# Block one's attention: from part-array float32 to full-array split float32r

## The chip, the core and the metric

The kernel runs on one core of one Trainium2 chip. What counts is the device time of one execution in microseconds; the median of three runs is compared. TensorE multiplies matrices out of SBUF into PSUM, VectorE, ScalarE and GpSimd (POOL) do the elementwise work, and SyncE (SP) issues nearly all DMAs from one in-order queue.

## What is computed

A network of two blocks on 512 tokens of 1024 features. The first block has two layers, and each runs five attention branches of 4 heads with 64 features beside one another: dsa (a top-256 mask over index scores), fox (forget gates in the logits), stick-breaking (sb), nsa (compressed, selected and window keys; with these sizes the selected and the window part see all causal keys) and mem (256 memory tokens). The branches are gated, merged and projected. The second block is not touched by the change.

```python
def _masked_softmax(logits, mask):
    l = jnp.where(mask, logits, -jnp.inf)
    m = jnp.max(l, axis=-1, keepdims=True)
    m = jnp.where(jnp.isfinite(m), m, 0.0)
    e = jnp.where(mask, jnp.exp(l - m), 0.0)
    return e / jnp.maximum(jnp.sum(e, axis=-1, keepdims=True), 1e-30)

def _fox_attention(q, k, v, log_f):
    ...
        logits = (jnp.einsum('bqhd,bshd->bhqs', q_blk, k).astype(jnp.float32) * scale
                  + jnp.moveaxis(c_blk, 1, 2)[..., None] - cum_s[:, :, None, :])
        mask = (s_pos[None, :] <= t[:, None])[None, None]
        p = _masked_softmax(logits, mask).astype(v.dtype)
        return jnp.einsum('bhqs,bshd->bqhd', p, v)

def _stick_breaking_attention(q, k, v):
    ...
        z = jnp.einsum('bqhd,bshd->bhqs', q_blk, k).astype(jnp.float32) * scale
        strict = (s_pos[None, :] < t[:, None])[None, None]
        log_keep = jnp.where(strict, jax.nn.log_sigmoid(-z), 0.0)
        later = lax.cumsum(log_keep, axis=3, reverse=True) - log_keep
        a = jnp.where(strict, jnp.exp(jax.nn.log_sigmoid(z) + later), 0.0).astype(v.dtype)
        return jnp.einsum('bhqs,bshd->bqhd', a, v)

def _layer(...):
    h = _rmsnorm(x, norm_g)
    p = _split_columns(h @ w_in)
    ...
    merge = jax.nn.sigmoid(p['merge'].reshape(B, S, N_BRANCH, D_MODEL))
    merged = jnp.sum(merge * jnp.einsum('bsnc,ncd->bsnd', ys, w_branch), axis=2)
    return x + merged @ w_out
```

## The kernel before

All work is written down as calls that a planner (`Plan`, L110) records. At `flush` (L363) it orders them by priority and by estimated costs (`cost`, L186), hands `ev` copies to VectorE or ScalarE and `tt` operations to VectorE or GpSimd, and emits each engine's fixed order; slots of tagged tiles are part of the plan. In the profile nearly every operation so recorded has line L119; copies and splits have L671 to L687.

Block one (`BlockOne.layer`, L1482) goes through the branches as mem, fox, sb, nsa, dsa. In a stage it writes down the attention of one branch (`*_a`), the projections of the next (`*_p`) and the gate and merge of the one before (`zm`, L1452), and `mix` (L283) spreads the priorities of attention and the rest over the same interval, so that projections stand between the attention's steps. Block two's conditioning products (`ada`) are spread in as well.

Projections are split already: weights and activations are cut into a float32r high part and a low part, and `mm3` (L745) adds three products of 128 rows by 128 columns. For each 512 KB weight tile `wraw` (four buffers) a high part `whi` is cast and a low part `wlo` subtracted, and the buffer is loaded again only after that.

The attention is float32. `softmax_branch` (L1125) takes a query tile of 128, and for each head `head` (L1087) forms the logits from 64 rows of q and k, adds mask rows, takes max, exponential, reciprocal and scale, turns the probabilities by transposes through PSUM and copies them to `pT`. `weigh` (L1118) multiplies 64 columns of v with `pT` for two heads, whose outputs lie in the two halves of the PSUM partitions. A float32 matmul leaves two records (passes) in the trace. `sb_a` (L1198) and `nsa_a` (L1402) have their own forms, `dsa_idx` (L1239) forms index scores from 32 rows a head. q, k and v of a branch lie in tiles of tag `qkv` (six slots); work tiles of 512 columns come from `t2` (12), and logits, turned tiles and outputs share five PSUM banks (`at`, L987).

Of the kernel before, what the change touches and what calls it, by code (L numbers as in the profile page):

```python
# [132 lines left out]
class Plan:  # L133
# [4 lines left out]
    def __init__(self, tc):  # L138
# [11 lines left out]
        self.kept = set()  # L150
        self.free = {e: 0.0 for e in "tsvgy"}
# [34 lines left out]
    def cost(self, eng, name, outs, ins, a, k):  # L186
        n = max(self.size(x) for x in outs[:1] + [y for y in ins if name in ("tensor_reduce", "max")])
        if eng == "t":
# [10 lines left out]
            if ins[0].dtype == F32R:  # L199
                return max(cols / 2.4, 107.0) + 2.5  # L200
# [23 lines left out]
    def add(self, alts, name, a, k):  # L224
# [24 lines left out]
        for ap, wr in [(x, False) for x in ins] + [(x, True) for x in outs]:  # L249
# [33 lines left out]
    def mix(self, *spans):  # L283

        a, b = min(x for x, _ in spans), max(y for _, y in spans)
        for x, y in spans:
            w = [o.alts[0][2] if o.alts[0][0] == "t" else 1.0 for o in self.ops[x:y]]
            tot, c = sum(w) or 1.0, 0.0
            for o, wi in zip(self.ops[x:y], w):
                o.prio = a + (b - a) * (c + 0.5 * wi) / tot  # L290
# [13 lines left out]
    def merge(self, ops):  # L304
# [48 lines left out]
        return out  # L353

# [285 lines left out]
class Net:  # L640
# [19 lines left out]
    nt2 = 12  # L660
# [49 lines left out]
    def wraw(self, src, m, n, tag="wraw", bufs=4):  # L710
        raw = self.wp.tile([P, 1024], F32, tag=tag, name="wraw", bufs=bufs)
# [197 lines left out]

class BlockOne:  # L910
# [7 lines left out]
    def run(self, xp, layers=DEPTH):  # L918
# [3 lines left out]
        self.xs = n.dr.tile([P, KD, S], F32, name="x_keep")  # L922
        with ExitStack() as ctx:
# [5 lines left out]
            n.pos_i = self.wk.tile([P, P], I32, tag="posi", name="pos_i", bufs=1)  # L929
            nc.sync.dma_start(n.pos_i[:NT, :P], I["positions"].rearrange("o (t p) -> (o t) p", p=P))  # L930
            for t in range(NT):
                r = self.qkv("x_in").rearrange("p a b -> p (a b)")
# [23 lines left out]
            self.c_cmp = self.const("cmp")  # L956
            self.negones = bp.tile([P, P], F32, tag="negones", name="negones")
# [55 lines left out]
    def mem_prep(self, wk):  # L1013

        n, nc, bp = self.n, self.nc, self.bp
        memT = [self.qkv("memT").rearrange("p a b -> p (a b)") for _ in range(2)]
        mt = lambda k: memT[k // 4][:, (k % 4) * NMEM:(k % 4 + 1) * NMEM]
# [15 lines left out]
        self.mem_k, self.mem_v = [], []  # L1033
        for l in range(DEPTH):
            hh = [self.qkv("memh", F32R).rearrange("p a b -> p (a b)") for _ in range(4)]
            class V:
                def __init__(s, a, b): s.t = (a, b)
                def __getitem__(s, i):
                    k, ts = i[1], i[2]
                    o = (k % 4) * NMEM  # L1040
                    return s.t[k // 4][:, o + ts.start:o + ts.stop]
            h = (V(hh[0], hh[1]), V(hh[2], hh[3]))
            for k in range(KD):
                m = n.t2("memg")[:, :NMEM]
                n.ev(m, mt(k), NMEM, scale=self.vcol(l, "mem_norm", k))
                sl = slice(0, NMEM)
                n.split(h[0][:, k, sl], h[1][:, k, sl], m, NMEM)
            w = self.I["w_mem_kv"][l]
            mk = bp.tile([P, 2, NMEM], F32, tag=f"memk{l}", name="mem_k")
            mv = bp.tile([P, 2, NMEM], F32, tag=f"memv{l}", name="mem_v")  # L1050
            for c, ps in n.proj_T(w[:, :256], h, slice(0, NMEM), 256):
                n.ev(mk[:, c], ps, NMEM)
            for t, ps in n.proj(w[:, 256:512], h, 256, range(2)):
                n.ev(mv[:, t], ps, 256)
            self.mem_k.append(mk)
            self.mem_v.append(mv)


    def pT(self, nm, h, dst, scale=None):
        n = self.n  # L1060
        o = OFF[nm]
        for c, ps in n.proj_T(self.w[:, o:o + 256], h, slice(0, S), 256):
            n.ev(dst[:, c], ps, 512, scale=scale)

    def qkv(self, nm, dt=F32):
        return self.bp.tile([P, 2, S], dt, tag="qkv", name=nm, bufs=6)

    def back(self, src_tiles, dst, scale=None):

        n, nc = self.n, self.nc  # L1070
        ps = self.tp()
        for t, s in enumerate(src_tiles):
            nc.tensor.transpose(ps[:, t * P:(t + 1) * P], s, n.ident)
        n.ev(dst, ps[:, :P * len(src_tiles)], P * len(src_tiles), scale=scale)

    def rope_T(self, w, h, dst, scale=None):
# [6 lines left out]
        for c in range(2):  # L1083
            self.back([r[:, t, c * P:(c + 1) * P] for t in range(NT)], dst[:, c], scale)


    def head(self, q, k, nk, mask, extra=None, gate=None):  # L1087
# [5 lines left out]
        nc.tensor.matmul(out, q, k, start=True, stop=mask is None and extra is None)  # L1093
# [14 lines left out]
        ps = self.tp()  # L1108
        for j in range(nk):
            nc.tensor.transpose(ps[:, j * P:(j + 1) * P], p[:, j * P:(j + 1) * P], n.ident)  # L1110
        pT = n.t2("pT")
        n.ev(pT[:, :N], ps[:, :N], N)
        return pT
# [4 lines left out]
    def weigh(self, pv, c, parts):  # L1118

        for x, (v, p, K) in enumerate(parts):  # L1120
            for i in range(2):
                self.nc.tensor.matmul(pv[64 * i:64 * i + 64, c * P:(c + 1) * P], v[i], p[i], start=x == 0,
                                      stop=x == len(parts) - 1, skip_group_check=True)

    def softmax_branch(self, q, k, v, yT, nk_of, mask_of, extra=None):  # L1125
        n = self.n
        for t in range(NT):
            nk = nk_of(t)
            pv = self.pv()
            ts = slice(t * P, (t + 1) * P)  # L1130
            for c in range(2):
                pT = [self.head(q[64 * i:64 * i + 64, c, ts], k(2 * c + i, nk), nk, mask_of(t),
# [1245 lines left out]
```

## Time and profile before

| | us |
|---|---|
| median of 3 runs (3393.59 to 3395.28) | 3395.07 |
| the profiled execution's own time | 3393.83 |
| its span, first to last instruction | 3392.0 |
| mean granted TensorE clock, share of full speed | 0.981 |

The profile is of one execution. Its page gives busy time by engine; a table by stretches gives the same for a piece of the span with the granted clock and the DMA share; the order of one engine's instructions gives start and duration of each, with equal neighbours merged. Matmuls overlap, so their durations are longer than the time that they occupy the array; start plus duration is the end, and the difference of two ends is the step. A shape such as 64*128 64x512 is rows and columns of the array in use, then the moving operand. float32r shows as f32 on matmuls.

### The profile page before, as it was taken

The page shows a single profiled execution, that of the slowest core. Times are in us where ns is not written, and L with a number is a line of the kernel's source. Part 1 is how long each engine was busy: PE and PEld are TensorE (multiplying, and loading weights), DVE is VectorE, ACT ScalarE, POOL GpSimd, SP SyncE. Part 2 cuts the span into 40 slices and gives each one's busy share as a digit, 9 for nine tenths or more (in the row PEclk, how much of TensorE's full clock was granted, in tenths as well). Part 3 has the DMA queues.
Part 4 walks back from the last instruction along what each step waited for, and adds up shares of the span by engine and source line. Part 5 has one row for each costly group of instructions (what it writes and reads, how often), then busy time and mean ns, then how long its engine had stood idle before and what let it go on. Part 6 is the DMA issues. An engine that isn't in the chain of part 4 may idle for free. (4 is left out here: it accounts for less than half of the span.)

```text
span 3392.0 us, 43819 instructions
## 1 busy us (share of the span) xinstructions
PE 3266.5 (96%) x16852; PEld 2496.3 (74%) x16856; DVE 2242.3 (66%) x4343; ACT 1123.3 (33%) x2548; POOL 242.3 (7%) x234
## 2 busy tenths in 40 slices
PE   7999999999999999999987899999999999989999
PEld 7677665677777666567775787888887777668887
DVE  8475855456665766445899977555557778775654
ACT  4333433212332433222321733111114666641112
POOL 1000100000000100000121100000000101110000
PEclk9999999999999999999998899999999999999999
DMA  6231421224232322123521231233222202133422
GB/s 184 77 92 40 126 70 52 58 79 126 57 88 68 101 67 73 46 73 94 167 75 56 82 94 57 90 91 100 86 61 76 64 20 78 48 95 92 117 75 88
DMA packets 378346, 278.21 MB, mean 82 GB/s; under 512 B 12172, under 2 KB 351384, under 8 KB 377880
## 3 DMA queue, kind: packets, MB, share of 16 engines
q1 hardware_dynamic: 378136, 275.40, 27.5%
q8 instruction: 133, 2.18, 0.3%
q14 instruction: 77, 0.63, 0.1%
HBM read 265.92 MB, written 9.44 MB: 81 GB/s over the span
## 5 line engine op out<-in xcount | busy, mean ns | idle before, releaser
L119 PE MATMUL ps_mm<-h_ffn,whi 128*128 128x512 f32 (+1 forms) x2112 | 566.3, 356 | 16.0 <-ACT h_ffn L119 8.0
L671 DVE CAST whi<-wraw 128x1024 fp32r<-128x1024 f32 (+7 forms) x339 | 199.3, 588 | 547.0 <-PE ps_mm L119 529.4
L687 DVE TENSOR_TENSOR wlo<-wraw,whi 128x1024 fp32r<-128x1024 f32 (+6 forms) x395 | 425.5, 1078 | 23.1 <-ACT whi L671 9.5
L119 PEld LDWEIGHTS ps_mm<-h_ffn,whi 128*128 128x128 f32 x2112 | 375.5, 190 | 78.0 <-ACT h_ffn L119 10.4
L119 PE MATMUL ps_mm<-hh,wlo 128*128 128x512 f32 x960 | 397.7, 414 | 0.9 <-DVE wlo L687 0.9
L119 PE MATMUL ps_mm<-hl,whi 128*128 128x512 f32 x960 | 396.1, 413 | 0.0
L119 PE MATMUL ps_mm<-hh,whi 128*128 128x512 f32 x960 | 393.9, 410 | 0.0
L119 PE MATMUL ps_mm<-h_ffn,wlo 128*128 128x512 f32 (+1 forms) x1056 | 374.4, 355 | 0.0
L119 DVE TENSOR_REDUCE mx<-ps_lg 128x1 f32<-128x384 f32 (+3 forms) x288 | 146.2, 509 | 156.2 <-PE ps_lg L119 135.8
L119 DVE CUSTOM_DVE_ANT_0 ada_junk<-wraw,cond,cols 128x1024 bf16<-128x1024 f32 x160 | 214.4, 1340 | 25.5 <-DMA wraw<-in_ada_wT_dram 24.9
L119 PEld LDWEIGHTS ps_mm<-hh,wlo 128*128 128x128 f32 x960 | 181.2, 189 | 59.1 <-issue 25.7
L119 PEld LDWEIGHTS ps_mm<-hh,whi 128*128 128x128 f32 x960 | 181.2, 189 | 58.6 <-issue 27.3
L119 PEld LDWEIGHTS ps_mm<-h_ffn,wlo 128*128 128x128 f32 x1056 | 200.4, 190 | 27.5
L119 PEld LDWEIGHTS ps_mm<-hl,whi 128*128 128x128 f32 x960 | 181.3, 189 | 52.0 <-issue 21.2
L119 ACT ACTIVATE p<-ps_lg,mx 128x384 f32<-128x384 f32 (+3 forms) x288 | 156.6, 547 | 163.0 <-DVE mx L119 161.6
L671 ACT COPY pT<-ps_tp 128x384 f32<-128x384 f32 (+3 forms) x244 | 105.0, 441 | 298.7 <-PE ps_tp L119 297.6
L119 PE MATMUL ps_mm<-fhi,wlo 128*128 128x512 f32 (+1 forms) x528 | 187.5, 357 | 0.0
L119 PE MATMUL ps_mm<-flo,whi 128*128 128x512 f32 (+1 forms) x528 | 186.7, 356 | 0.0
L119 PE MATMUL ps_mm<-fhi,whi 128*128 128x512 f32 (+1 forms) x528 | 186.4, 355 | 0.0
L671 ACT COPY gpad<-ps_mm 128x512 f32<-128x512 f32 x64 | 33.4, 523 | 429.9 <-PE ps_mm L119 429.3
L671 ACT CAST whi<-wraw 128x1024 fp32r<-128x1024 f32 (+8 forms) x122 | 114.5, 940 | 175.2 <-PE ps_mm L119 111.9
L687 POOL TENSOR_TENSOR wlo<-wraw,whi 128x256 fp32r<-128x256 f32 (+4 forms) x66 | 107.7, 1634 | 878.4 <-DVE whi L671 472.3
(519 smaller groups left out, 6425.9 us busy)
## 6 DMA issues: line engine op xcount, KB each, us to landing
wraw<-in_w_in_dram SPq DMA_DIRECT2D x132, 512.0 KB
wraw<-in_ada_wT_dram SPq DMA_DIRECT2D x96, 512.0 KB
wraw<-in_ffn_w_in_dram SPq DMA_DIRECT2D x88, 512.0 KB
wraw<-in_ffn_w_out_dram SPq DMA_DIRECT2D x64, 256.0 KB
wraw<-in_w_branch_dram SPq DMA_DIRECT2D x20, 512.0 KB
wraw<-in_w_out_dram SPq DMA_DIRECT2D x16, 512.0 KB
wraw<-in_ab_w_in_dram SPq DMA_DIRECT2D x16, 512.0 KB
x_keep<-xT SPq DMA_DIRECT2D x3, 2048.0 KB
```

The source lines that it names most:

```text
L119: return plan.add([(eng, lambda: fn(*a, **k))], name, a, k)
L671: self.plan.either("tensor_copy", {"v": lambda x: x.tensor_copy(out, in_), "s": lambda x: x.copy(out, in_)}, out, in_)
L687: f = lambda x: x.tensor_tensor(out, a, b, op=op)
```

## The change

q and k of every branch are stored as a stack: for each head, 64 rows of high part and under them 64 rows of low part, in float32r. A second copy of k with the halves swapped (`swapped`, two DMAs of 128 KB a head from SBUF to SBUF) lets two products over 128 rows give all four partial products, and `head` and `sb_a` do so. v is stored as 64 high and 64 low columns, so one product over 128 columns gives both halves, and `out_pair` adds them. The turned probabilities are cut into high and low parts straight from PSUM, for two query tiles side by side (`pair`, `sets`, `weigh`); keys that only the second tile sees take 128 columns, the others 256. Index scores and compressed logits take the same form. The branches run heads outside and tile pairs inside.

Storage follows: tag `st` has 8 slots of 4 KB a partition, and a branch takes two each for q, k and v; `t2` goes from 12 to 8; mem keys and values of the second layer go to DRAM and come back, as do the index scores. `zm` is written down in two halves, one ahead of the next projections and one behind, `mix` gives attention priorities over 0.7 of the interval, and `towards` lets the planner hold a projection until its target slots are free. The planner's cost of a float32r matmul is changed as well.

```diff
-                return max(cols / 2.4, 107.0) + 2.5
+                return max(cols / 2.255, 107.0) + 2.5
...
+        if alts[0][0] == "t":
+            tiles += [x.tensor.name for x in self.into if x.tensor.name not in tiles]
...
+                o.prio = a + (b - a) * (1.0 if (x, y) != spans[0] else lead) * (c + 0.5 * wi) / tot
...
-    nt2 = 12
+    nt2 = 8
...
+    def slot(self, nm, dt=F32R):
+        return self.bp.tile([P, 2, S], dt, tag="st", name=nm, bufs=8)
...
+    def stack(self, dst, c, ps, scale=1.0):
+
+        n = self.n
+        N = ps.shape[1]
+        for i in range(2):
+            src = ps[64 * i:64 * i + 64]
+            hi = dst[c][0:64, i, :N]
+            n.ev(hi, src, N, scale=None if scale == 1.0 else scale)
+            self.nc.vector.scalar_tensor_tensor(dst[c][64:P, i, :N], src, scale, hi.bitcast(F32),
+                                                op0=ALU.mult, op1=ALU.subtract)
...
+    def split_v(self, dsts, ps):
+
+        src = ps.rearrange("p (h d) -> p h d", d=64)
+        o = 0
+        for dst in dsts:
+            H = dst.shape[1]
+            x = src[:, o:o + H]
+            self.n.ev(dst[:, :, :64], x, 64 * H)
+            self.nc.vector.tensor_tensor(dst[:, :, 64:], x, dst[:, :, :64].bitcast(F32), op=ALU.subtract)
+            o += H
...
+    def swapped(self, k1, h):
+
+        k2 = self.bp.tile([P, S], F32R, tag="k2", name="k2", bufs=3)
+        for a, b in ((0, 64), (64, 0)):
+            self.nc.sync.dma_start(k2[a:a + 64].bitcast(F32), k1[h // 2][b:b + 64, h % 2].bitcast(F32))
+        return k2
...
-        nc.tensor.matmul(out, q, k, start=True, stop=mask is None and extra is None)
+        nc.tensor.matmul(out, q, ks[0][:, :N], start=True, stop=False)
+        nc.tensor.matmul(out, q, ks[1][:, :N], start=False, stop=mask is None and extra is None)
...
+    def pair(self, t0, nk_of, head):
+
+        n = self.n
+        hl = self.parts("pT")
+        for u in range(2):
+            nk = nk_of(t0 + u)
+            src = head(t0 + u, nk)[:, :nk * P].rearrange("p (j q) -> p j q", q=P)
+            hi, lo = (x[:, :nk, u * P:(u + 1) * P] for x in hl)
+            n.ev(hi, src, nk * P)
+            self.nc.vector.tensor_tensor(lo, src, hi.bitcast(F32), op=ALU.subtract)
+        return hl, nk_of(t0 + 1), nk_of(t0)
+
+    def weigh(self, pv, i, sets):
+
+        flat = [(v, p, a) for v, hl, a in sets for p in hl]
+        for x, (v, p, a) in enumerate(flat):
+            self.nc.tensor.matmul(pv[:, i * 256 + a:(i + 1) * 256], v, p, start=x == 0, stop=x == len(flat) - 1,
+                                  skip_group_check=True)
+
+    def sets(self, v, hl, keys, full):
+        return [(v(j), [x[:, j, (0 if j < full else P):] for x in hl], 0 if j < full else P) for j in range(keys)]
 
     def pv(self):
         return self.at("ps_pv")
 
-    def weigh(self, pv, c, parts):
-
-        for x, (v, p, K) in enumerate(parts):
...
+    def out_pair(self, yT, c, t0, pv):
+
+        n, nc = self.n, self.nc
+        lo = n.t2("pv_lo")
+        nc.scalar.copy(lo[64:P], pv[64:P])
+        for i in range(2):
+            cols = slice(i * 256, (i + 1) * 256)
+            nc.vector.tensor_tensor(yT[64 * i:64 * i + 64, c, t0 * P:(t0 + 2) * P], pv[0:64, cols], lo[64:P, cols], op=ALU.add)
+
...
+    def softmax_branch(self, q, keys, v, yT, nk_of, mask_of, extra=None):
+        for c in range(2):
+            ks = [keys(2 * c + i) for i in range(2)]
+            for t0 in (0, 2):
+                pv = self.pv()
+                for i in range(2):
+                    h = 2 * c + i
+                    hl, nk, full = self.pair(t0, nk_of, lambda t, nk: self.head(
+                        self.hd(q, h)[:, t * P:(t + 1) * P], ks[i], nk, mask_of(t), extra(h, nk) if extra else None))
+                    self.weigh(pv, i, self.sets(lambda j: v[c][:, j, i], hl, nk, full))
+                self.out_pair(yT, c, t0, pv)
...
+                    hl = [x.rearrange("p j q -> p (j q)")[:, :N] for x in self.parts("sb_aT")]
+                    n.split(hl[0], hl[1], a, N)
+                    for y, x in enumerate(hl):
+                        nc.tensor.matmul(pv[i][:, s0:], v[c][:, s, i], x, start=s == NT - 1 and y == 0, stop=s == 0 and y == 1,
+                                         skip_group_check=True)
...
-                nc.tensor.matmul(lg, qi[hh * 32:hh * 32 + 32, t * P:(t + 1) * P], ki[hh * 32:hh * 32 + 32, :N],
-                                 start=True, stop=True)
+                nc.tensor.matmul(lg, self.hd(qi, hh)[:, t * P:(t + 1) * P], ki[:, :N], start=True, stop=True)
...
+            nc.sync.dma_start(self.scores[:, t, :N], sc[0])
...
+                for h in range(4):
+                    for x in range(2):
+                        nc.tensor.matmul(lg[:, h * 32:(h + 1) * 32], self.hd(q, h)[:, t * P:(t + 1) * P], kc[x], start=x == 0, stop=x == 1)
...
+            if d == 3:
+                yield
...
+            zm = self.zm(BRANCHES.index(seq[i - 1]), h, ys[seq[i - 1]], acc, i == 1) if i else iter(())
+            next(zm, None)
...
+            next(zm, None)
             if i + 1 < len(seq):
                 nx = seq[i + 1]
                 st[nx] = self.dsa_p(h, ckv) if nx == "dsa" else getattr(self, nx + "_p")(h)
...
```

## Rows read from the trace of the kernel before

**Rows 1.** The page's first part: busy us, share of the span, instructions.

```profile
PE 3266.5 (96%) x16852; PEld 2496.3 (74%) x16856; DVE 2242.3 (66%) x4343; ACT 1123.3 (33%) x2548; POOL 242.3 (7%) x234
```

**Rows 2.** Table by stretches: length, busy us (instructions), clock, DMA share, GB/s.

```profile
20.00:1612.00 1592.00, 1565.11 (x7510) 1094.94 (x7515) 966.84 (x1927) 510.43 (x1112) 100.97 (x84) 0.99 0.28 81
320.00:420.00 100.00, 96.30 (x466) 66.94 (x465) 80.77 (x152) 46.08 (x74) 14.95 (x16) 1.00 0.37 104
420.00:820.00 400.00, 397.32 (x1803) 267.79 (x1805) 217.23 (x421) 109.24 (x258) 18.05 (x12) 1.00 0.25 71
1800.00:2000.00 200.00, 168.85 (x935) 139.68 (x935) 185.97 (x409) 95.07 (x297) 16.20 (x8) 0.85 0.22 70
2640.00:3000.00 360.00, 354.18 (x2226) 258.89 (x2224) 274.71 (x767) 228.98 (x655) 43.62 (x67) 1.00 0.17 54
```

**Rows 3.** TensorE's order around 237 us: start, us, operation, tiles, shape, records merged.

```profile
236.24 0.40 PE L119 MATMUL ps_mm<-hh,wlo 128*128 128x512 f32 x1
236.56 1.12 PE L119 MATMUL ps_lg<-fox_k,fox_q 64*128 64x512 f32 x2
...
237.62 0.50 PE L119 MATMUL ps_mm<-hh,whi 128*128 128x512 f32 x1
237.95 0.40 PE L119 MATMUL ps_mm<-hl,whi 128*128 128x512 f32 x1
```

**Rows 4.** The same view around 85 us.

```profile
85.12 0.40 PE L119 MATMUL ps_mm<-hl,whi 128*128 128x512 f32 x1
85.45 0.70 PE L119 MATMUL ps_lg<-mem_k,mem_q 64*128 64x256 f32 x2
```

**Rows 5.** The same view around 524 us.

```profile
523.73 0.40 PE L119 MATMUL ps_mm<-hl,whi 128*128 128x512 f32 x1
524.06 0.87 PE L119 MATMUL ps_pv<-pT,nsa_v 128*64 128x128 f32 x10
524.86 0.50 PE L119 MATMUL ps_mm<-hh,wlo 128*128 128x512 f32 x1
```

**Rows 6.** The same view: first and last of 475 records behind a part-array matmul.

```profile
44.48 0.55 PE L119 MATMUL ps_tp<-ident,mem_in 128*128 128x128 f32 x3
...
1502.23 0.50 PE L119 MATMUL ps_br<-yh,wlo 128*128 128x512 f32 x1
```

**Rows 7.** Views of ps_lg and ps_pv: records, ns min/median/max, first and last start.

```profile
L119 PE MATMUL ps_lg<-nsa_k,nsa_q x128: 272/481/693, 446.3 to 1382.9; 64*128 64x128 f32 x32, 64*128 64x256 f32 x32, 64*128 64x384 f32 x32, 64*128 64x512 f32 x32
...
L119 PE MATMUL ps_pv<-pT,nsa_v x320: 272/273/324, 461.7 to 1400.0; 128*64 128x128 f32 x160
```

**Rows 8.** TensorE's order around 158 and 183 us, short float32r matmuls.

```profile
158.29 0.40 PE L119 MATMUL ps_mm<-hh,wlo 128*128 128x512 f32 x1
158.53 0.22 PE L119 MATMUL ps_lg<-cum_parts,pick 128*128 128x128 f32 x1
158.59 0.23 PE L119 MATMUL ps_lg<-causalb,identb 128*128 128x128 bf16 x1
158.63 0.31 PE L119 MATMUL ps_lg<-cum_parts,pick 128*128 128x128 f32 x1
...
183.03 0.28 PE L119 MATMUL ps_mm<-whi,hh 128*128 128x256 f32 x1
183.15 0.28 PE L119 MATMUL ps_mm<-wlo,hh 128*128 128x256 f32 x1
```

**Rows 9.** VectorE's order around 533 us; its weight casts up to 1650 us.

```profile
533.25 0.56 DVE L119 TENSOR_REDUCE mx<-ps_lg 128x1 f32<-128x384 f32 x1 [0.27 <-PE ps_lg L119]
533.72 0.68 DVE L687 TENSOR_TENSOR acc<-acc,gt 128x512 f32<-128x512 f32 x1
534.32 0.15 DVE L119 TENSOR_TENSOR sm<-sm,nsa_v 128x1 f32<-128x1 f32 x1
...
L671 DVE CAST whi<-wraw 128x1024 fp32r<-128x1024 f32 x128 | 89.4, 698 | 243.7 <-PE ps_mm L119 231.7 <-PE ps_br L119 9.4 <-issue 2.4
```

**Rows 10.** Waits of the SP queue: waited for, us in total, times, longest.

```profile
SPq L119 <- DVE wlo L687: 1702.2, 331, 26.6
```

More of the change, by code (lines that the diff above doesn't have):

```diff
@@ L353, in merge, with towards @@
         return out
+    def towards(self, *aps):
+        self.into = aps
     def keep(self, *aps):
@@ L1045, in mem_prep @@
                 n.ev(m, mt(k), NMEM, scale=self.vcol(l, "mem_norm", k))
-                sl = slice(0, NMEM)
-                n.split(h[0][:, k, sl], h[1][:, k, sl], m, NMEM)
+                n.split(h[0][:, k, every], h[1][:, k, every], m, NMEM)
             w = self.I["w_mem_kv"][l]
[L1049 to L1052, printed above, removed]
+            mk, mv = self.mem_tiles()
@@ L1060, in pT @@
+    def pT(self, nm, h, dst, scale=1.0):
         n = self.n
         o = OFF[nm]
+        n.plan.towards(dst[0])
         for c, ps in n.proj_T(self.w[:, o:o + 256], h, slice(0, S), 256):
[L1063 to L1070, printed above, removed]
+            self.stack(dst, c, ps, scale)
+            n.plan.towards(*dst[1 + c:])
@@ L1083, in rope_T, with head @@
         for c in range(2):
-            self.back([r[:, t, c * P:(c + 1) * P] for t in range(NT)], dst[:, c], scale)
-    def head(self, q, k, nk, mask, extra=None, gate=None):
+            n.plan.towards(dst[c])
+            self.stack(dst, c, self.turn([r[:, t, c * P:(c + 1) * P] for t in range(NT)]), scale)
+        n.plan.towards()
+    def head(self, q, ks, nk, mask, extra=None, gate=None):
         n, nc, wk = self.n, self.nc, self.wk
@@ L1107, in head, with parts @@
         n.scale_rows(p, sm)
[L1108 to L1113, printed above, removed]
+        return self.turn([p[:, j * P:(j + 1) * P] for j in range(nk)])
+    def parts(self, nm):
+        return [self.wk.tile([P, 4, 2 * P], F32R, tag=x, name=nm, bufs=self.nparts) for x in ("ph", "pl")]
+    nparts = 2
+    def pair(self, t0, nk_of, head):
[8 more added lines that the diff above has]
+        return hl, nk_of(t0 + 1), nk_of(t0)
@@ L1202, in sb_a @@
         for c in range(2):
-            pv = self.pv()
-            off = [0, 512, 896, 1152]
-            at = [wk.tile([P, 1280], F32, tag="sba", name="sb_a", bufs=2) for _ in range(2)]
+            k2 = [self.swapped(k, 2 * c + i) for i in range(2)]
+            pv = [self.pv() for _ in range(2)]
             later = [n.t2("sb_later") for _ in range(2)]
@@ L1244, in dsa_idx @@
         wi = bp.tile([P, NT, 4], F32, tag="wi", name="idx_w")
-        qr = wk.tile([P, NT, 256], F32, tag="rq", name="idx_r", bufs=1)
+        qr = [n.t2("idx_r").rearrange("p (h c d) -> p h c d", h=4, c=4) for _ in range(NT)]
+        kr = wk.tile([P, NT, 256], F32, tag="rq", name="idx_kr", bufs=1)
         for t, ps in n.proj(self.w[:, o:o + 292], h, 292, range(NT)):
@@ L1304, in dsa_kv @@
             n.tt(r[:, t].rearrange("p (h d) -> p h d", d=64), a, b, ALU.add, 256)
-            n.ev(v[:, t], ps[:, 256:], 256)
+            self.split_v([x[:, t] for x in v], ps[:, 256:])
         for c in range(2):
-            self.back([r[:, t, c * P:(c + 1) * P] for t in range(NT)], k[:, c])
+            n.plan.towards(k[c])
+            self.stack(k, c, self.turn([r[:, t, c * P:(c + 1) * P] for t in range(NT)]))
+        n.plan.towards()
         return k, v
@@ L1523, in layer @@
                 plan.spread(self.topk, self.topk[0], a0)
-        self.zm(BRANCHES.index(seq[-1]), h, ys[seq[-1]], acc, False)
+        for _ in self.zm(BRANCHES.index(seq[-1]), h, ys[seq[-1]], acc, False):
+            pass
         mh = bp.tile([P, KD, S], F32R, tag="hh", name="mh")
```

320 lines of the change are left out of this document (181 added, 139 removed).

## The prediction

> **What bounds the kernel now.** I read the page's first part, then the table by stretches, then TensorE's order of work. TensorE is busy 96% of the span, VectorE 66%, ScalarE 33% [rows 1]. The change touches block one alone, which runs from about 10 us to 1612 us: there TensorE is busy 1565 of 1592 us at a granted clock of 0.99, which is its 2.4 GHz level, while VectorE is busy 967 and ScalarE 510 [rows 2]. So block one is bound by TensorE's own work, and its time changes with that work as long as the other engines keep feeding it.
>
> What that work costs is read from ends of matmuls, not from their durations, which overlap: the step from the end of one record to the end of the next. Full-array projections of 512 columns step by 0.23 us (from 238.12 to 238.35) [rows 3]. The old attention is dearer than its arithmetic in three ways.
>
> - Logits run on 64 rows in float32, two passes each. The pair with 512 columns ends 1.04 us after the projection before it (236.64 to 237.68) [rows 3], the pair with 256 columns 0.63 us after (85.52 to 86.15) [rows 4]. So 256 columns more cost a pair 0.41 us, 512 columns 0.82, and about 0.22 is the price of entering.
> - After such a pair the next projection of 512 takes 0.44 us and not 0.23 (237.68 to 238.12) [rows 3]. After a run of 64-column products of probabilities and values (ps_pv) it is the same: 0.43 us (524.93 to 525.36) [rows 5].
> - A run of 10 ps_pv passes takes 0.80 us (524.13 to 524.93) [rows 5], entering included, with the two heads' column halves side by side.
>
> Such an exit to the full array occurs 475 times, from 44.5 us to 1502.2 us [rows 6].
>
> **What the change removes.** There are 384 logit passes (nsa 128, and mem, fox, dsa and stick-breaking 64 each, by rows of the same view as [rows 7]), 192 pairs: 40 each of 128, 384 and 512 columns, 72 of 256. On the line through the two measured pairs they cost 0.42, 0.63, 0.84 and 1.05 us: 16.8 + 45.4 + 33.6 + 42.0 = 138 us. The 896 ps_pv passes (nsa 320 [rows 7], fox and dsa 160 each, mem 128, stick-breaking and compressed nsa 64 each), their steps summed over all records, take 130 us. The index scores (48 passes) and compressed logits (64) take 26 us in the same count. The 475 exits at 0.19 us, the mean over all of them, are 89 us. Sum: 383 us.
>
> **What it puts in their place on TensorE.** Every product becomes a full-array float32r one, so entries and exits go. Steps: 0.23 us for 512 columns [rows 3], 0.12 for 256 [rows 8], 0.176 for 384 on the line between. For 128 columns there are two prices: 0.06 us where a long matmul stands before (158.69 to 158.75) and 0.11 to 0.12 where a short one does (158.82 to 158.94) [rows 8]; I take 0.115, since the new ones come in runs. The Trainium skill ("TensorE: Matmul & The Clock Gate", "LDWEIGHTS") says a weight load takes its columns over 1.2, an estimated 0.107 us for 128, which would bind such runs; the rows behind short matmuls agree, and by the rule the sum stays as it is made below and the 16 us of its lower bound don't come.
>
> Per layer: logits are two products a tile, 2 x (0.115 + 0.12 + 0.176 + 0.23) = 1.28 us a head, for 20 causal heads (fox, dsa, stick-breaking 4 each, nsa 8) 25.6; mem 32 x 0.12 = 3.8; index 4 x 0.53 = 2.1; compressed 32 x 0.115 = 3.7. Values, two query tiles at once: a causal head has 8 products of 256 columns and 4 of 128, 1.42 us, for 16 heads 22.7; mem 3.8; stick-breaking 4 x 1.28 = 5.1; compressed 1.0. Twelve more transposes for the index at 0.11: 1.3. That is 69 us a layer, 138 in both. Bounds: at 0.06 for all 288 products of 128 columns it is 16 us less; the dear end is the sum itself, because no full-array row shows more. Net: 383 - 138 = **245 us less TensorE work**.
>
> **What it adds elsewhere.** A VectorE instruction on 512 columns occupies the engine 0.60 us (533.72 to 534.32), on 384 0.47 (533.25 to 533.72) [rows 9]; on that line 0.34 for 256 and 0.20 for 128. Per layer: low parts of probabilities, 16 x 1.61 + 16 x 0.34 = 31 us; low parts of q and k, 16 tensor halves x 2 x 0.60 = 19, with nsa and mem keys 22; of v 6; stick-breaking's split 10; the two-half adds on the way out 13; index and compressed parts 8. About 90 us a layer, 180 in both; some may go to ScalarE or GpSimd. ScalarE gains about 20 a layer. So VectorE has 967 + 180 = 1147 us to do beside 1592 - 27 - 245 = 1320 us of TensorE work, of which 89 us of weight casts can move to ScalarE [rows 9]. All of this lies beside TensorE's work; without that cover 1147 us is still less than 1320.
>
> Hidden altogether: the copies of swapped halves (12 heads a layer in fox, stick-breaking and dsa, two copies of 128 KB each) and of mem keys, values and scores, some 6 MB a layer where 81 GB/s at a share of 0.28 flow now [rows 2]. They queue on SP with the weight loads, and SP mostly waits for the low-part subtraction of weights (1702 us in all, longest 26.6) [rows 10]. Behind a copy that waits for VectorE's stack stand weight loads, and behind those the projections; four raw buffers, each 24 products of 0.23 = 5.5 us, are the cover. The new order of the merge (half ahead of the next projections, attention at 0.7 of the stage) costs no instruction.
>
> **The waits that come back.** This is the unknown. TensorE's idle share against VectorE's busy share: 0.7% at 54%, 1.7% at 61%, 1.6% at 76%, 15.6% at 93% (there the clock also fell to 0.85 of 2.4 GHz) [rows 2]. Block one would stand at 76 to 83%, and unevenly: a stretch at 81% today (320 to 420 us) [rows 2] gains VectorE work and loses TensorE work. I take 5.5% of 1320 + waits, about 75 us, where 27 are now: 48 us given back. The ends are 0 and the 15.6% row, 1320 x 0.185 = 244 - 27 = 217.
>
> So the span falls by 245 - 48 = 197. The profiled execution took 3393.83 us for a span of 3392.0, 0.04% under the median of 3395.07; 3393.8 - 197 = **3197 us**.
>
> **The rivals.** *VectorE becomes the bound* in the attention stages. For it: 81% at 320 to 420 us already, one in-order queue in which a new subtraction stands behind weight subtractions over 1024 columns, and a transposed tile that now stays in PSUM until two readers are done. Against: the average of 76 to 83%. Price: waits as at 1800 to 2000 us, 217 more, so a gain of 28 and 3366 us; from 131 us more on, 3280, I count it as this rival. By the Trainium skill ("TensorEngine Tiling (Array Packing)", "PSUM Bottleneck") a faster TensorE can make the PSUM copies the bottleneck; no row here shows it on this stage, and it would act as this rival does.
>
> *The copies block SP.* Each of 24 heads' swapped keys waits for a stack, and the weight loads behind starve the projections. The change ends slower once a head's copy costs more than 245/24 = 10.2 us of idle TensorE; with 20 us, below SP's longest wait of 26.6 [rows 10], it is 3393.8 - 245 + 480 = 3629 us. Against: raw buffers cover 22 us of projection, and SP's wait is mostly room, not need.
>
> *Nothing comes back*: waits stay at 27 us and 128-column products hide their loads: 3393.8 - 261 = 3133 us.
>
> **How the numbers follow.** Forecast 0.75 (3150 to 3280), VectorE bound 0.14 (3280 to 3370), nothing back 0.07 (3133 to 3150), SP blocked 0.04 (above 3400). The range 3145 to 3285 takes in the forecast and the near edges of its neighbours. Faster by over 0.2% (6.8 us, about what a measurement of this kernel tells from no change): 0.95; within 0.2%: 0.01; slower: 0.04.
>
> **What would show it.** Right: no records of 64 rows or 64 columns under ps_lg, ps_z and ps_pv before block two; a projection right behind ps_pv stepping 0.23; block one ending near 1415 us; TensorE idle there for 60 to 90 us, before projections that wait for wlo and before transposes that wait for p. VectorE busy there about 1100 us. Wrong: VectorE above 90% over 300 us with TensorE idle beside it, or TensorE waiting for swapped keys. A 128-column float32r run stepping well off 0.115, or a full-array product that keeps an exit of 0.19 behind it, would make the sum itself wrong.

## The result, and the profile after

The changed kernel takes 3293.5 us (median of four runs, 3291.6 to 3294.7) against 3394.7 for the kernel before on the same chip: a ratio of 0.970, 95% interval 0.9685 to 0.9718. It is faster by 101 us where 197 were forecast, and lies 8.5 us above the upper end of the range.

The page of after, first part, busy us and share of the span, as [rows 1]:

```profile
PE 3081.8 (94%) x16488; PEld 2520.2 (77%) x16488; DVE 2391.8 (73%) x4762; ACT 1177.7 (36%) x2633; POOL 325.1 (10%) x281
```

TensorE is busy 185 us less and VectorE 150 us more, and the span fell by 102, from 3392.0 to 3289.8. The table by stretches, columns as in [rows 2] (after the length: TensorE, its weight loads, VectorE, ScalarE, GpSimd, then clock, DMA share, GB/s):

```profile
20.00:1500.00 1480.00, 1376.08 (x7137) 1115.77 (x7138) 1113.81 (x2338) 568.83 (x1200) 178.59 (x130) 0.97 0.34 94
300.00:420.00 120.00, 103.68 (x572) 85.06 (x572) 94.37 (x197) 59.71 (x102) 17.27 (x20) 0.93 0.26 74
420.00:580.00 160.00, 148.29 (x813) 120.03 (x812) 127.42 (x312) 65.81 (x164) 16.12 (x14) 0.98 0.31 84
580.00:720.00 140.00, 140.00 (x663) 112.72 (x663) 88.45 (x151) 37.21 (x80) 8.63 (x4) 1.00 0.31 85
```

In block one TensorE stands idle for 1480.00 - 1376.08 = 104 us, where 27 stood before [rows 2], and unevenly: nothing from 580 to 720 us, 16 us from 300 to 420, at a clock of 0.93. Where block one ends is read from the last product of its last projection in TensorE's order (start, duration):

```profile
1509.00 0.39 PE L119 MATMUL ps_mm<-mh,wlo 128*128 128x512 f32 x1
```

It ends at 1509.4 us, where it ended at 1619.2 before; block one gained 110 us and the rest of the program lost 8 (1772.8 to 1780.4); those 8 were not followed up.

The following table adds up the steps between the ends of all TensorE records of block one, against what the same form costs where nothing is waited for (0.23 us for 512 columns, as in [rows 3]). Late steps are the difference: waits, and steps stretched by the lower clock.

| us in block one | before | after | change | forecast |
|---|---|---|---|---|
| the attention's steps on part of the array | 292.7 | 0 | | |
| its exits back to the full array, 475 | 90.1 | 0 | -383 together | -383 |
| attention on the full array | 46.0 | 179.9 | +134 | +138 |
| all other full-array work | 1110.5 | 1113.1 | +3 | 0 |
| late steps | 79.8 | 216.3 | +136 | +48 |
| sum | 1619.1 | 1509.4 | -110 | -197 |

The few part-array products of the set-up and of nsa's compression, which both kernels have, are in the fourth row.

So the sum of TensorE's work was right to 2%, and the term of the waits that come back was not: 136 us in place of 48. Only 77 of the 136 are idle time of TensorE (27 to 104); in the other 59 it counts as busy. Part of those is the clock: by the trace's clock records block one spent 85 us at the 1.2 GHz level, 27 before. The full-speed work that stood in these intervals is, by the same steps, an estimated 34 and 11 us, so the slower clock itself costs by this estimate some 20 us more than before. The experiments ask what the 136 us hang on.

### The profile page after: what moved, and what is told of

The parts are those of the page before. It is cut to its first block, busy times and chain, and to the rows that moved or that the text cites. A ratio compares the mean times of both kernels' runs of the same rounds, so it can differ in the third digit from the quotient of the medians.

```text
span 3289.8 us, 43893 instructions
## 1 busy us (share of the span) xinstructions
PE 3081.8 (94%) x16488; PEld 2520.2 (77%) x16488; DVE 2391.8 (73%) x4762; ACT 1177.7 (36%) x2633; POOL 325.1 (10%) x281
## 4 chain that ended last, share of the span: by engine, by line
PE 40%; DVE 10%; ACT 1%; issue 1%; DMA 1%; POOL 0%; ACTq 0%; DVEq 0%; POOLq 0%; SPq 0%
PE ps_mm L119 32%; DVE u L119 4%; PE ps_lg L119 2%; PE ps_tp L119 2%; PE ps_pv L119 2%; DVE ada_junk L119 1%; DVE y_mod L119 1%; PE ps_nd L119 1%; PE ps_st L119 1%; DVE dm L119 0%; DVE h_ffn L119 0%; DMA wraw<-in_ab_w_in_dram 0%; DVE sq L119 0%; DMA wraw<-in_ffn_w_in_dram 0%; DVE xT L119 0%
## 5 line engine op out<-in xcount | busy, mean ns | idle before, releaser
L679 DVE CAST whi<-wraw 128x1024 fp32r<-128x1024 f32 (+7 forms) x317 | 185.3, 585 | 453.8 <-PE ps_mm L119 441.5
L695 DVE TENSOR_TENSOR wlo<-wraw,whi 128x1024 fp32r<-128x1024 f32 (+4 forms) x359 | 379.1, 1056 | 21.3 <-ACT whi L679 9.5
L119 PE MATMUL ps_mm<-hh,wlo 128*128 128x512 f32 x960 | 389.2, 405 | 0.2 <-DVE wlo L695 0.2
L119 PE MATMUL ps_mm<-hl,whi 128*128 128x512 f32 x960 | 388.7, 405 | 0.0
L695 POOL TENSOR_TENSOR wlo<-wraw,whi 128x1024 fp32r<-128x1024 f32 (+6 forms) x102 | 187.4, 1839 | 1099.6 <-DVE whi L679 572.9
L119 PEld LDWEIGHTS ps_mm<-h_ffn,wlo 128*128 128x128 f32 x1056 | 200.6, 190 | 27.7
L679 ACT CAST whi<-wraw 128x1024 fp32r<-128x1024 f32 (+8 forms) x144 | 135.8, 944 | 227.1 <-PE ps_mm L119 161.2
L679 ACT COPY gpad<-ps_mm 128x512 f32<-128x512 f32 (+1 forms) x63 | 32.8, 520 | 399.7 <-PE ps_mm L119 399.0
L119 PE MATMUL ps_tp<-ident,p 128*128 128x128 f32 x768 | 133.3, 278 | 12.3 <-ACT p L691 5.9
```

What stands on the lines that cost most here:

```text
L119: return plan.add([(eng, lambda: fn(*a, **k))], name, a, k)
L679: self.plan.either("tensor_copy", {"v": lambda x: x.tensor_copy(out, in_), "s": lambda x: x.copy(out, in_)}, out, in_)
L695: f = lambda x: x.tensor_tensor(out, a, b, op=op)
```

## Experiments

Three theories were set against each other. *VectorE*: the waits come from VectorE's amount of work. *Order*: the waits come where no independent product is next in TensorE's fixed order while a chain of dependent steps runs (maximum, exponential, reciprocal, scale, transposes, high part, low part). *Queue*: the copies of swapped keys hold up the weight loads. One place in the profile of after shows the difficulty of telling the first two apart. TensorE's order (start, duration, records; in brackets the idle time before and its releaser):

```profile
339.74 0.22 PE L119 MATMUL ps_z<-sb_q,sb_k 128*128 128x128 f32 x1
...
340.32 0.28 PE L119 MATMUL ps_mm<-whi,hl 128*128 128x256 f32 x1
342.90 0.49 PE L119 MATMUL ps_z<-sb_later,c_suffix 128*128 128x128 f32 x2 [2.30 <-DVE sb_later L695]
...
343.33 0.36 PE L119 MATMUL ps_mm<-whi,hh 128*128 128x256 f32 x1
```

and VectorE's at the same time:

```profile
339.80 0.28 DVE L119 TENSOR_SCALAR sb_e<-ps_z 128x128 f32<-128x128 f32 x1
340.11 0.68 DVE L119 TENSOR_TENSOR yT<-ps_pv,pv_lo 64x512 f32<-64x512 f32 x1
340.82 1.28 DVE L119 CUSTOM_DVE_ANT_0 ada_junk<-wraw,cond,cols 128x1024 bf16<-128x1024 f32 x1
...
342.03 0.28 DVE L119 TENSOR_TENSOR sb_e<-ps_z,sb_e 128x128 f32<-128x128 f32 x1
...
342.57 0.28 DVE L695 TENSOR_TENSOR sb_later<-sb_e,c_strict 128x128 f32<-128x128 f32 x1
342.77 0.42 DVE L119 TENSOR_TENSOR rope_b<-ps_mm,ss 128x256 f32<-128x256 f32 x1
```

and ScalarE's:

```profile
343.54 0.28 ACT L119 ACTIVATE sb_a<-ps_z 128x128 f32<-128x128 f32 x1 [2.78 <-PE ps_z L119]
...
345.13 0.60 ACT L119 ACTIVATE gt<-ps_mm 128x512 f32<-128x512 f32 x1
```

TensorE waits 2.30 us for `sb_later`. VectorE is busy throughout, and of the chain only 0.28 us each: the sb_e of 342.03 stood behind a conditioning product of 1.28 us that has nothing to do with it. That speaks for VectorE. The projection products of 343.33, which stand right behind in TensorE's order and need nothing from that chain, could not have filled the gap: projections, gates and merges share three PSUM tiles (`psm`), and all three were taken. One held a gate whose products had ended at 333.8 and which ScalarE read at 345.13, one a merge that VectorE read at 346.57, and one the projection before, until `rope_b` had read it at 343.19. ScalarE stood idle for 2.78 us before 343.54, with the gate behind an exponential of the chain in its queue. That speaks for the order, but for the order of all the engines' queues and not of TensorE's alone.

All runs, with the idle time of TensorE and VectorE's busy share from the table by stretches over block one (20 us to about 9 us before its end), and the clock there. These last four columns are of the profiled execution, whose time is up to 8 us from the median (lead1 3440.5, merge_first 3278.4). The ratios are to the kernel before on the same chip; runs sent at different times are compared by them.

| run | us | ratio, 95% interval | block one ends | TensorE idle | VectorE busy | clock |
|---|---|---|---|---|---|---|
| kernel before | 3394.7 | 1 | 1619 | 27 | 61% | 0.99 |
| changed kernel | 3293.5 | 0.9702 (0.9685 to 0.9718) | 1509 | 104 | 75% | 0.97 |
| lead1 | 3448.7 | 1.0166 (1.0149 to 1.0183) | 1663 | 201 | 71% | 0.92 |
| merge_first | 3271.7 | 0.9646 (0.9631 to 0.9660) | 1498 | 90 | 77% | 0.96 |
| topk1 | 3277.0 | 0.9654 (0.9640 to 0.9669) | 1496 | 91 | 71% | 0.96 |
| lo_zero | 3282.3 | 0.9678 (0.9663 to 0.9692) | 1501 | 92 | 73% | 0.96 |
| before_new_order | 3396.2 | 1.0007 (0.9998 to 1.0017) | 1627 | 40 | 60% | 0.97 |
| same_keys | 3288.5 | 0.9696 (0.9680 to 0.9712) | 1510 | 105 | 75% | 0.97 |
| merge_first87 | 3240.2 | 0.9548 (0.9534 to 0.9562) | 1458 | 73 | 78% | 0.98 |
| warm | 3273.5 | 0.9649 (0.9633 to 0.9665) | 1486 | 84 | 77% | 0.98 |
| no_claim | 3274.4 | 0.9649 (0.9634 to 0.9663) | 1496 | 92 | 76% | 0.97 |
| whole_merge | 3294.1 | 0.9703 (0.9689 to 0.9718) | 1511 | 98 | 76% | 0.96 |
| topk1_87 | 3231.5 | 0.9522 (0.9506 to 0.9537) | 1452 | 69 | 74% | 0.98 |
| stages | 3243.5 | 0.9558 (0.9542 to 0.9574) | 1460 | 72 | 78% | 0.98 |
| light | 3229.1 | 0.9510 (0.9494 to 0.9526) | 1441 | 59 | 67% | 0.98 |
| at4 | 3259.6 | 0.9598 (0.9584 to 0.9612) | 1477 | 77 | 77% | 0.97 |
| longer | 3266.6 | 0.9623 (0.9609 to 0.9638) | 1482 | 84 | 77% | 0.98 |

### The order alone, with the instructions kept

**lead1** puts one number back.

```diff
-LEAD = 0.7
+LEAD = 1.0
```

> The changed kernel with one number put back: the attention of a stage is spread over the whole stage again (1.0 and not 0.7 of it). All instructions stay, only their order moves. Order theory (waits come where no independent products are left to stand between the dependent steps of the attention): slower than the changed kernel by 60 to 150 us, 3350 to 3440 us, with TensorE waiting for the probabilities' row scaling (p) at the ends of stages. VectorE theory (waits come from VectorE's total work, which is the same): within 15 us of 3293.

It takes 3449 us, 155 more than the changed kernel, a little above the order theory's range, and 1.7% more than the kernel before: with the attention spread over the whole stage, all of the 249 us of TensorE work saved are lost again, and some more. The table by stretches and TensorE's waits (total us, times, longest):

```profile
20.00:1655.00 1635.00, 1434.36 (x7134) 1153.42 (x7143) 1158.08 (x2374) 576.35 (x1202) 156.89 (x114) 0.92 0.30 85
```

```profile
PE ps_tp L119 <- DVE p L690: 55.2, 41, 5.5
...
PE ps_tp L119 <- ACT p L691: 14.9, 18, 2.7
...
PE ps_z L119 <- DVE sb_later L695: 8.5, 5, 3.0
```

Idle TensorE 200.6 us, clock 0.92, VectorE busy 1158 of 1635 us, a lower share than in the changed kernel. In the changed kernel p from VectorE costs 4.0 us in 7 waits (below), here 55.2 in 41. One such wait, first TensorE, then VectorE, then ScalarE:

```profile
571.69 0.33 PE L119 MATMUL ps_lg<-causalb,identb 128*128 128x128 bf16 x1
573.74 1.09 PE L119 MATMUL ps_tp<-ident,ckv 128*128 128x128 f32 x4 [1.72 <-DVE ckv L119]
577.27 0.66 PE L119 MATMUL ps_tp<-ident,p 128*128 128x128 f32 x2 [2.45 <-DVE p L690]
```

```profile
572.91 0.68 DVE L119 TENSOR_TENSOR ckv<-ckv,ckv_ss 128x512 f32<-128x512 f32 x1
576.25 0.16 DVE L119 RECIPROCAL sm<-sm 128x1 f32<-128x1 f32 x1 [2.66 <-ACT p L119]
...
576.64 0.48 DVE L690 TENSOR_SCALAR p<-p,sm 128x512 f32<-128x512 f32 x1
```

```profile
574.86 0.69 ACT L685 ACTIVATE ckvT<-ps_tp,cols 128x512 f32<-128x512 f32 x1 [2.19 <-PE ps_tp L119]
575.44 0.68 ACT L119 ACTIVATE p<-ps_lg,mx 128x512 f32<-128x512 f32 x1
```

From 574.83 to 577.27 TensorE has nothing, and VectorE waits too, 2.66 us for ScalarE's exponential. The exponential stood behind the copy `ckvT`, which itself had waited 2.19 us for TensorE's transposes. No engine is short of time; two chains go from engine to engine, and no products lie between. The VectorE theory, by which the time follows from VectorE's amount of work and so could not change by over 15 us, falls here.

**merge_first** goes the other way: the whole merge stands ahead of the next projections, and the claim that makes a projection take its slots early is off.

```diff
-        self.into = aps
+        self.into = ()
...
-            next(zm, None)
+            for _ in zm:
+                pass
             if i + 1 < len(seq):
```

> The changed kernel with the whole merge of the branch before put ahead of the next branch's projections (not half of it), and without the early claim on the slots of the stacked tiles; all instructions stay. Order theory: faster than the changed kernel by 15 to 60 us, 3233 to 3278 us, since products of the merge are there when the chains of the next projections run. VectorE theory: within 15 us of 3293.

22 us faster (19 by the ratios), inside what the order theory gave. **no_claim** and **whole_merge** make the two halves of that edit, one each:

> The changed kernel without the early claim on the slots of the stacked tiles, one half of what the run with the merge ahead changed; half the merge stays ahead. All instructions stay. Order theory, if the claim holds projections back: 10 to 25 us faster than the changed kernel (3293 us), 3268 to 3283; if the place of the merge is what counts: within 8 us of 3293. VectorE theory: within 8 us.

> The changed kernel with the whole merge ahead of the next projections, the early claim kept: the other half. Order theory, if the place of the merge is what counts: 10 to 25 us faster than the changed kernel, 3268 to 3283; if the claim is: within 8 us of 3293. VectorE theory: within 8 us.

Without the claim 18 us are gained (by the ratios, 0.9649 against 0.9702), with the whole merge ahead nothing (0.9703). So it was the claim. **merge_first87** then sets LEAD = 0.87 on merge_first:

> The run with the merge ahead, its attention spread over 0.87 of the stage and not 0.7; instructions are the same. Order theory: 0 to 25 us faster than that run (3272 us), 3247 to 3272, because with the merge ahead the stage's end has the chains of the next projections, and attention steps left there give them cover. VectorE theory: within 10 us of 3272.

3240 us, 31 less than merge_first (33 by the ratios) and more than expected, and, level with stages below, the fastest kernel here that leaves nothing out: 1.6% below the changed kernel and 4.5% below the kernel before. Its table by stretches and waits:

```profile
20.00:1450.00 1430.00, 1357.10 (x7141) 1103.10 (x7142) 1116.83 (x2336) 572.26 (x1213) 165.04 (x127) 0.98 0.34 97
```

```profile
PE ps_tp L119 <- ACT p L691: 7.8, 10, 1.6
...
PE ps_z L119 <- POOL sb_later L695: 5.7, 9, 1.3
...
PE ps_z L119 <- DVE sb_later L695: 2.3, 3, 1.1
...
PE ps_tp L119 <- DVE p L690: 2.0, 2, 1.8
...
PE ps_tp L119 <- DVE roped L695: 1.3, 2, 0.6
```

TensorE idle 73 us in place of 104, at the highest VectorE share of all runs. In the changed kernel the same view reads:

```profile
PE ps_z L119 <- DVE sb_later L695: 11.7, 8, 2.7
PE ps_tp L119 <- DVE roped L695: 10.1, 7, 2.0
PE ps_mm L119 <- ACT hh L679: 6.2, 2, 3.3
...
PE ps_tp L119 <- DVE p L690: 4.0, 7, 1.2
...
PE ps_pv L119 <- DVE pT L119: 3.6, 8, 0.9
```

The waits for VectorE's sb_later and roped have gone from 21.8 us to 3.6 (from 24.9 to 10.7 with those that GpSimd makes); what is left is spread thin. Whether 0.87 would do as well with the claim or with half a merge was not tried. **stages** sets LEAD to 0.80, 0.82, 0.87, 0.80 and 0.82 by stage:

> The run with the merge ahead, the share of the stage over which the attention is spread chosen for each of the five stages: 0.80, 0.82, 0.87, 0.80 and 0.82 in place of 0.87 for all. Instructions are the same. Order theory: between the runs with 0.70 and with 0.87 for all or somewhat below them, 3225 to 3265 us. VectorE theory: as the run with 0.87, within 10 us of 3240, and as the run with 0.70, which two cannot both be.

3244 us, no better than 0.87 for all. From lead1 to merge_first87 the same operations take 3449 or 3240 us.

**before_new_order** gives the kernel before the change's LEAD of 0.7 and its half merge, and keeps its attention.

> The kernel before with only the order of the change: the attention spread over 0.7 of its stage, half of the merge ahead of the next projections; the old attention stays, with its part-array products. Order theory (the new order is worth something only because the new attention waits for its probabilities more often per us of TensorE work): within 40 us of the kernel before, 3375 to 3435 us, since only some 50 us of waits stand there. If the order alone were the gain of the change, it would come out 80 to 110 us faster, 3285 to 3315 us.

```profile
20.00:1618.00 1598.00, 1557.61 (x7506) 1111.98 (x7507) 966.12 (x1928) 506.45 (x1114) 83.23 (x72) 0.97 0.27 80
```

No gain: 1.0007. Exits fall from 475 to 389, 14 us less, and late steps rise by 29. This order is worth something only with the new attention.

### VectorE's work

**topk1** leaves out 15 of 16 rounds of the key selection, `for r in range(1)`. **lo_zero** leaves out the low parts of the softmax probabilities and lets the second product of each pair read zeros (and stick-breaking has one buffer for low parts, not two):

```diff
...
-            self.nc.vector.tensor_tensor(lo, src, hi.bitcast(F32), op=ALU.subtract)
-        return hl, nk_of(t0 + 1), nk_of(t0)
+        return [hl[0], self.zero], nk_of(t0 + 1), nk_of(t0)
```

> The changed kernel with one round of the key selection in place of 16, which leaves out 15 of 16 pairs of maximum and replacement: about 106 us less VectorE work in block one (113.6 us of it in the profile of the changed kernel, times 15/16), none of it in the chain that TensorE waits for stage by stage, TensorE's work the same; other keys are masked. VectorE theory: faster than the changed kernel by 50 to 106 us, 3187 to 3243 us. Order theory: 0 to 15 us faster.

> The changed kernel with the low parts of the softmax probabilities left out: their products stay, but read a tile of zeros. That takes 160 subtractions from VectorE, 75 us by their durations, and one step from each head's chain, and a transposed tile in PSUM has one reader less to wait for. VectorE theory: faster than the changed kernel by 40 to 75 us, 3218 to 3253 us, like the run with less key selection in proportion to the work removed. Order theory: faster by 5 to 30 us, more per us of VectorE work than with less key selection, because the step lies in the chain.

The table by stretches of topk1:

```profile
20.00:1488.00 1468.00, 1376.57 (x7134) 1123.20 (x7143) 1042.07 (x2100) 558.98 (x1191) 153.97 (x109) 0.96 0.33 95
```

topk1 gained 16 us by the ratios, lo_zero 8 (11 by the medians). VectorE's busy time fell by 72 us in topk1, not by 106, since the planner hands it work that ScalarE and GpSimd had done (they fall by 10 and 25). Per us left out that is 0.15 and 0.11 (of 106 and 75 us), alike within the intervals: that the step in the chain weighs more than the same work outside it, which the order theory had expected, is not seen.

**topk1_87** repeats topk1 on merge_first87, and **light** leaves out there, besides, the low parts and the conditioning products beside block one.

> The run with the attention over 0.87 of its stage and the merge ahead, with one round of the key selection in place of 16 (15 of 16 pairs of maximum and replacement left out): about 106 us less VectorE work in block one, as in the first such run. If VectorE's amount of work is what is left once the order is better: 40 to 100 us faster than that run (3240 us), 3140 to 3200. Order theory: 0 to 20 us faster, 3220 to 3240, as the 16 us on the changed kernel.

> The run with the attention over 0.87 of its stage and the merge ahead, with VectorE's work cut in three places: the low parts of the softmax probabilities (a tile of zeros is read), 15 of 16 rounds of the key selection, and the modulation products of block two that are made beside block one (a constant in their place) are left out. Together about 245 us (75 + 106 + 64 by durations) of some 1117 us of VectorE work in block one; TensorE's work is the same. VectorE theory (what is left of the waits comes from VectorE's amount): block one loses most of its remaining 85 us of extra waits, 60 to 100 us faster than that run (3240 us), 3140 to 3180. Theory of chain and cover: 10 to 40 us faster, 3200 to 3230.

```profile
20.00:1433.00 1413.00, 1353.76 (x7134) 1108.86 (x7143) 941.06 (x1876) 546.55 (x1178) 127.17 (x93) 0.98 0.36 99
```

topk1_87 is 9 us faster than merge_first87, light 13 (by the ratios, 0.9548 to 0.9522 and 0.9510); in light block one itself ends 17 us earlier. With VectorE busy 941 us and not 1117 (ScalarE loses 26 and GpSimd 38 more), TensorE is still idle for 59 us, and the late steps of block one fall from 165 to 150. VectorE's amount is not what most of the waits hang on.

### The chain, the PSUM tiles, the copies, the clock

**longer** adds one step to each of the 160 head chains of merge_first87, on ScalarE; **at4** leaves it four PSUM tiles, not five.

```diff
-        return self.turn([p[:, j * P:(j + 1) * P] for j in range(nk)])
+        p2 = n.t2("p_again")[:, :N]
+        nc.scalar.copy(p2, p)
+        return self.turn([p2[:, j * P:(j + 1) * P] for j in range(nk)])
```

> The run with the attention over 0.87 of its stage and the merge ahead, with one more dependent step in each of the 160 head chains: ScalarE copies the scaled probabilities once more before they are transposed (about 0.4 us each on average, 65 us on ScalarE, which is busy 39% there; no VectorE work). Theory of chain and cover: slower than that run (3240 us) by 10 to 40 us. VectorE theory: within 8 us of 3240.

> The run with the attention over 0.87 of its stage and the merge ahead, with four PSUM tiles in place of five for the attention's logits, transposes and values; the fifth bank stays empty. If the tiles in PSUM, held until both readers are done, are what the remaining waits hang on: slower than that run (3240 us) by 30 us or more. Theory of chain and cover: within 20 us of 3240.

The table by stretches of longer, and the first of its TensorE's waits:

```profile
20.00:1474.00 1454.00, 1370.44 (x7134) 1111.52 (x7143) 1120.97 (x2333) 639.75 (x1379) 161.03 (x122) 0.98 0.34 95
```

```profile
PE ps_tp L119 <- ACT p_again L119: 22.2, 22, 2.3
```

longer costs 25 us by the ratios, though ScalarE is busy only 640 of 1454 us and VectorE does no more than in merge_first87: twice what 240 us less work gained in light (by the ends of block one 24 against 17 us). TensorE's transposes wait 22.2 us for the added copy, where they waited 12.1 for the probabilities in merge_first87. The copy also takes ScalarE's time and one of the eight work tiles of `t2`; what these cost was not separated. at4 costs 17 us, under the 30 that would have made the tiles the cause. The Trainium skill ("Perfetto Trace Analysis", "Optimization Strategy") says that repeated gaps on the engine that should be full can mean too little SBUF or PSUM for the next tile; at4 agrees in sign, with 17 us.

**same_keys** reads the first key tile twice (`self.hd(k, h)` in place of `self.swapped(k, h)`), which leaves the copies and the logits' cross terms out.

> The changed kernel without the swapped-half copies of the keys: the second product of each logit reads the first tile of keys again, so 48 copies of 64 x 512 are left out and the logits lack their cross terms; every engine's other work stays. Theory of the blocked queue (weight loads stand behind copies that wait for VectorE): faster than the changed kernel by 15 us or more. Order theory: within 10 us of 3293.

5 us by the medians, 2 by the ratios. SP's waits for VectorE's low part of the weights over the whole run, first in the changed kernel, then in same_keys:

```profile
SPq L119 <- DVE wlo L695: 1358.6, 291, 29.3
```

```profile
SPq L119 <- DVE wlo L695: 1416.7, 296, 29.3
```

They do not grow with the copies; both are below those of the kernel before [rows 10]. The queue theory falls.

**warm** puts 226 products of 128 columns into the waits that the planner foresees in merge_first.

> The run with the merge ahead, and in each wait that the planner foresees for TensorE in block one, products of 128 columns of an identity tile in bfloat16, written to the PSUM tile that the next instruction overwrites. They add no result. Clock theory (about 90 us of block one's excess lie in intervals at the 1.2 GHz level that follow waits, and work in the waits keeps the clock up): 15 to 50 us faster than that run (3272 us), 3222 to 3257, with fewer us at the low level. If the intervals at the low level do not come from the waits, or the added products push out real ones: 0 to 30 us slower.

```profile
20.00:1478.00 1458.00, 1374.18 (x7367) 1118.22 (x7368) 1124.08 (x2341) 574.18 (x1214) 154.37 (x123) 0.98 0.33 95
```

Time at the 1.2 GHz level in block one fell from 116 us in merge_first to 61; the added products took 15 us of steps. Block one ends 12 us earlier, but the two profiled executions differ by 9 us the same way (3278.4 and 3269.1), and the medians are the same (3273.5 and 3271.7). So the low clock follows the waits here, and filling them with empty work wins nothing that the medians show.

## Why the prediction was right or wrong

**TensorE's sum: right.** Removed 383 us as forecast, put in 134 and not 138. The 128-column products of logits and values keep the two prices of [rows 8]: a median step of 0.06 us right behind a longer product, 0.11 behind another short one, at the 2.4 GHz level; 0.115 was taken for all, but over half of them stood behind a longer one. The rule of the Trainium skill ("TensorE: Matmul & The Clock Gate", "LDWEIGHTS"), an estimated 0.107 us for 128 columns, agrees with the second and not with the first. The attention's exits are gone: a projection behind a logit or behind seven products of values ends 0.23 or 0.29 us after them, not 0.43 and 0.44 as in [rows 3, 5].

```profile
600.85 0.39 PE L119 MATMUL ps_mm<-hl,whi 128*128 128x512 f32 x1
601.07 0.34 PE L119 MATMUL ps_lg<-dsa_k,dsa_q 128*128 128x384 f32 x1
601.25 0.39 PE L119 MATMUL ps_mm<-hh,wlo 128*128 128x512 f32 x1
...
604.02 0.40 PE L119 MATMUL ps_br<-yl,whi 128*128 128x512 f32 x1
604.25 0.92 PE L119 MATMUL ps_pv<-pT,dsa_v 128*128 128x256 f32 x7
605.01 0.45 PE L119 MATMUL ps_br<-yh,wlo 128*128 128x512 f32 x1
```

(601.41 to 601.64, and 605.17 to 605.46.)

**VectorE's work: right.** Forecast 1147 us, or about 1100 after the casts that move; 1114 were measured. What moved was mostly not the casts (15 us fewer on VectorE) but the weights' subtractions (42 us fewer, taken by GpSimd), and the fullest 300 us in the table by stretches (800 to 1100) held 250, 83%.

**The waits that come back: wrong, and this is the whole miss.** The step that failed is the line from VectorE's busy share to TensorE's idle share through [rows 2], 5.5% at 76 to 83%. At 75% it is 104 of 1480 us, 7%. Of the 88 us beyond the forecast 48 that makes 29; the other 59 are late steps in which TensorE counts as busy, at the low clock or in small delays, and the sum had no term for them, because it read waits from idle time alone. And there is no such line: over the runs, idle time goes from 201 us at 71% to 73 at 78% and 59 at 67%. The four stretches of before had different stages in them, and the share was a companion of the idle time, not its cause. What the line could not see, by the account that fits these runs best, is that the work taken away had been cover. Before, each head's chain ran beside 429 us of the attention's own TensorE time (292.7 + 90.1 + 46.0), beside other heads' slow logits and values; after, beside 180, with one step more in the chain, the low part. That this is why the waits came back, and why lead1 loses all that the change saves, is argued from the sums; shown is that the order alone moves 208 us, and that a longer chain costs about twice what 240 us less VectorE, ScalarE and GpSimd work gains.

**The rivals.** VectorE as the bound was to be counted from 3280 us on, and the time lies there, but as an amount of work it is refuted by topk1 and light. The in-order queue that this rival named is what the place at 342.03 us shows, and how much of the 136 us it makes was not measured. The blocked queue is refuted by same_keys; its point of decision, 10.2 us a head, was never near. *Nothing comes back* was wrong by 136 us. The rival that was missing is lead1's: chains with too little beside them, which end slower than before at the spread of 1.0 that the kernel before had.

**The signs named.** No 64-row records in the attention, no exits from it, VectorE about 1100: as said. Block one's end, 1415 foreseen, was 1509. TensorE's idle time, 60 to 90 us foreseen, was 104, and not before projections that wait for `wlo`, but in the chains of stick-breaking, rope and the probabilities.

**Left open.** merge_first87 still has 165 us of late steps against 80 before. longer shows that they respond to the chain's length, at4 that they respond to the attention's PSUM tiles; how the 85 divide between these was not measured, nor was a chain with fewer steps tried alone on that kernel. Which engine's order counts was not separated, since LEAD moves all of them. The three PSUM tiles of the projections, which held them back at 343 us, and the work tiles (12 before, 8 after) were not varied.

## What to carry to other kernels

When work is taken from the engine that bounds, ask what waited behind that work: it may have been cover for somebody's chain, and the order that fitted it has to be made anew (one number, LEAD, moved this kernel by 4.7%). Price the waits from a chain's length against the independent work that stands beside it, stage by stage, and not from the busy share of another engine; and count late steps, not idle time alone. Before blaming an engine, take work from it: 176 us less on VectorE brought 13.

## What the hardware showed that was not expected

The granted clock fell where TensorE waited more: lead1, with 201 us of idle time, ran at a mean of 0.92 in block one, merge_first87 with 73 at 0.98, and products put into merge_first's waits took its time at the 1.2 GHz level from 116 to 61 us. A 128-column full-array product in float32r steps by 0.06 us right behind a longer one and by 0.11 behind another short one.
